# The recurrence's state enters the PSUM sum through a product with the identity, instead of a scaled copy on ScalarE

## Chip, core and metric

The kernel runs on one core of one Trainium2 chip. The metric is the device time of one execution in microseconds (us), the median of several runs. PE is TensorE's matmul, PEld its weight load, DVE is VectorE, ACT is ScalarE, POOL is GpSimd, SP is SyncE.

## What is computed

One layer of a hybrid decoder over 1024 prompt tokens and 8 single-token samples: norm, one input projection, a pooling mixer and an RWKV-7 recurrence side by side, one output projection, norm, a squared-ReLU MLP, a final norm. The part that matters here is the recurrence, for each of 8 heads of 64 x 64 state:

```
def step(S, inp):
    r_t, w_t, k_t, v_t, aa_t, bb_t = inp
    sa = jnp.einsum('bhvk,bhk->bhv', S, aa_t)
    S = S * w_t[:, :, None, :] + sa[..., None] * bb_t[:, :, None, :] + v_t[..., None] * k_t[:, :, None, :]
    return S, jnp.einsum('bhvk,bhk->bhv', S, r_t)
S_final, y = lax.scan(step, S0, xs)
```

## The kernel before

The prompt is worked in units: a unit is a pair of heads (`hp`, 0 to 3) in one half of the tokens (512), so 8 units. For each unit `rkv` projects the keys, receptances and values (line 185, tile `pj`: products in a high and a low part, three matmuls for each), `stage1` (S) makes the decays and the score matrices (line 431, tile `sc`), `inverse` (I) inverts the eight 64 x 64 triangular matrices of the unit's chunks by DVE, a trip through DRAM (`blk`, `inv`, `TX`) and small PE products (lines 548 to 570, tile `pi`) into `TT`, and `chain` (C) runs the recurrence itself: 8 chunks of 64 tokens, one after the other, 64 chunk steps in the whole kernel.

A chunk step in `chain` (lines 592 to 617 of the listing) goes through four engines in turn. `SV` holds for each head the state in one half of the partitions and the values in the other.

- PE, line 601: `pq` = AR x SV; line 602 starts the output sum `py`.
- ACT, `act(Q, pq)`: copies `pq` to SBUF.
- PE, line 605: `pa` = TT x Q.
- ACT, `act(SV[R[h], c, h, :], pa...)`, twice: puts the result over the state in SV.
- PE, line 608: `pu` = BKT x SV (the same PSUM columns as `pq`); line 609 ends `py`.
- DVE, line 617, twice: the next state = `pu` x gam + `sg`, written into the next chunk's SV.

`sg`, the old state times the chunk's decay `gam`, is made by ACT at the head of the step (line 596), before the state is overwritten. Products of full fp32 operands, as all of these, are two weight loads and two matmuls each on PE.

A Tile scheduler puts the instructions of all stages in an order on each engine, by priorities and by its own estimate of the costs; `lead_chain` gives the chain a lead of 600 places in that order. Each engine then runs its list strictly in order. So projections of later units stand between the products of a chunk step on PE. SP issues the loads in its own order (`TX` is the inverse on its way back, `mr` loads the mixer's rows for the output projection), POOL's queue issues the weights and the stores of mixer rows. After the last unit come the decode step, the output projection (`mx`, line 185 again) and the MLP.

Of the kernel before, what the change touches and what calls it, by code (L numbers as in the profile page):

```python
# [7 lines left out]
F32 = mybir.dt.float32  # L8
F32R = mybir.dt.float32r
AF = mybir.ActivationFunctionType  # L10
ALU = mybir.AluOpType
# [4 lines left out]
P = 128  # L16
# [70 lines left out]
def _build(ctx, nc, tc, I, O, dbg):  # L87
    V, A, PE, SY, GP = nc.vector, nc.scalar, nc.tensor, nc.sync, nc.gpsimd
# [4 lines left out]
    def act(out, in_, func=AF.Copy, bias=0.0, scale=1.0, **k):  # L93
        A.activation(out, in_, func, bias=bias, scale=scale, **k)  # L94

    def open_pool(stack, name, bufs=1, **k):
        return stack.enter_context(tc.tile_pool(name=name, bufs=bufs, **k))

    R = (slice(0, 64), slice(64, 128))
# [13 lines left out]
    ident = cst[:, C_ID:C_ID + 128]  # L113
# [77 lines left out]
    rcp = open_pool(st_left, "rcp", reuse_waits="tile")  # L191
# [386 lines left out]
    def chain(U):  # L578
        hp = U.hp
        z1 = Zt[U.half][2]  # L580
        for i in range(2):
            nm = f"{hp}_{2 * U.half + i}"
            AR, RB, BKT, SV, TT = U.AR[i], U.RB[i], U.BKT[i], U.SV[i], U.TT
            if i == 0:
                for h in range(2):
                    if U.half == 0:
                        GP.memset(SV[R[h], 0, h, :], 0.0)
                    else:
                        act(SV[R[h], 0, h, :], Sf[hp][R[h], :])
            pyp = ps_y.tile([P, 512], F32, tag="y", name=f"py{nm}")  # L590
            py = pyp.rearrange("p (c h t) -> p c h t", h=2, t=64)
            for c in range(4):
                g = 4 * i + c
                gn = f"{U.nm}_{g}"
                sg = rcp.tile([P, 2, 64], F32, tag="sg", name=f"sg{gn}", bufs=2)
                act(sg, SV[:, c, :, :], scale=U.gam[:, g:g + 1])

                o = 256 * (hp % 2)
                pq, pa = (pcs[:, o + 128 * q:o + 128 * q + 128].rearrange("p (h t) -> p h t", t=64) for q in range(2))
                pu = pq  # L600
                PE.matmul(pq, AR[:, c, 0, :, :], SV[:, c, :, :], start=True, stop=True)  # L601
                PE.matmul(py[:, c, :, :], SV[:, c, :, :], AR[:, c, 1, :, :], start=True, stop=False)
                Q = rcp.tile([P, 2, 64], F32, tag="Q", name=f"Q{gn}", bufs=2)
                act(Q, pq)
                PE.matmul(pa, TT[:, g, :, :], Q, start=True, stop=True)  # L605
                for h in range(2):
                    act(SV[R[h], c, h, :], pa[R[h], h, :])
                PE.matmul(pu, BKT[:, c, :, :], SV[:, c, :, :], start=True, stop=True)  # L608
                PE.matmul(py[:, c, :, :], SV[:, c, :, :], RB[:, c, :, :], start=False, stop=True)
                for h in range(2):  # L610
                    if g == 7:
                        dst = Sf[hp][R[h], :]
                    elif c == 3:
                        dst = U.SV[1][R[h], 0, h, :]
                    else:
                        dst = SV[R[h], c + 1, h, :]
                    V.scalar_tensor_tensor(dst, pu[R[h], h, :], U.gam[R[h], g:g + 1], sg[R[h], h, :], ALU.mult, ALU.add)
            ys = rcp.tile([P, 256], F32, tag="ys", name=f"ys{nm}", bufs=2)
            for h in range(2):
                act(ys[R[h]].rearrange("p (c t) -> p c t", t=64), py[R[h], :, h, :])  # L620
            post(hp, nm, pyp, ys, 256, U.bv[:, 256 * i:256 * i + 256], z1[:, 256 * i:256 * i + 256], ys)
            QM.dma_start(mix_d[4 + hp][U.half][:, 256 * i:256 * i + 256], ys)
        if U.half:
            QM.dma_start(O["wkv_p"][hp], Sf[hp])

    def post(hp, nm, ps, ys, n, bv, zg, out):

        pm, pv = ps[:, 256:512], ps[:, 0:256]
        PE.matmul(pm[:, :n], CJ, ys, start=True, stop=True)
        q = rcp.tile([P, 256], F32, tag="q", name=f"q{nm}", bufs=1)  # L630
        act(q[:, :n], pm[:, :n], AF.Square)
        PE.matmul(pv[:, :n], BO, q[:, :n], start=True, stop=True)
        act(q[:, :n], pv[:, :n], AF.Ln, bias=EPSG, scale=1.0 / 64)
        act(q[:, :n], q[:, :n], AF.Exp, scale=-0.5)
        V.tensor_tensor(out, pm[:, :n], q[:, :n], op=ALU.mult)
        V.scalar_tensor_tensor(out, out, col(V_LG, hp), bv, ALU.mult, ALU.add)
        pg = pm
        PE.matmul(pg[:, :n], glu[:, hp * P:(hp + 1) * P], zg, start=True, stop=True)
        V.scalar_tensor_tensor(out, out, col(V_LB, hp), pg[:, :n], ALU.add, ALU.mult)
# [184 lines left out]
    def lead_chain(U):  # L824
        with tc.high_priority(offset=LEAD):
            chain(U)
# [313 lines left out]
    for b in (1, 2):  # L1140
        c, n = BLK[b]
# [88 lines left out]
```

## Time and profile before

| | us |
|---|---|
| median of 3 runs (lowest, highest) | 1336.54 (1336.04, 1337.41) |
| the profiled execution | 1335.81 |
| its span in the trace | 1334.0 |
| busy in the span: PE, PEld, DVE, ACT | 1267.3, 1146.4, 1050.9, 822.5 |
| first and last chunk step in the span | 67.5 to 521 |

The table's busy times overlap each other. A matmul's end is modelled and neighbours overlap, so a PE that reads as busy can still have room; the distance from one weight load to the next is the better measure of what a product takes of PE's time. In the trace's rows a bracket behind an instruction says how long its engine had been idle before it and what ended that.

### The profile page before, as it was taken

The numbers are of one execution on the slowest core, as the hardware profiler recorded it, in microseconds if no ns is written. First come the engines' busy times: TensorE is split into PE (matmuls) and PEld (weight loads), VectorE is DVE, ScalarE is ACT, GpSimd is POOL, SyncE is SP. The second block draws the span as 40 slices with busy tenths as digits, with TensorE's granted clock in tenths as the row PEclk, the third lists the DMA queues.
The fourth block names the chain that finished last, engine by engine and source line by source line (L and its number), as shares of the span: only waits on it lengthen the run. The fifth ranks groups of instructions, "written<-read, shape, count | busy, mean of one in ns | idle before, by whom it ended". The sixth has DMA issues, their size and how long they took to land.

```text
span 1334.0 us, 27179 instructions
## 1 busy us (share of the span) xinstructions
PE 1267.3 (95%) x10230; PEld 1146.4 (86%) x10230; DVE 1050.9 (79%) x2331; ACT 822.5 (62%) x2015; POOL 125.4 (9%) x248
## 2 busy tenths in 40 slices
PE   5999999899999989989999999999899999999996
PEld 5987788798777867789989888998799999999996
DVE  8897687778877756589989997786698787878775
ACT  7668677776777657364757564555465645455552
POOL 4101001210011021110002320001000000000000
PEclk9999999999999989999999999999899999999999
DMA  6323123222222253442335663335634323332321
GB/s 209 102 54 83 43 50 90 95 93 53 66 56 48 63 164 135 142 149 80 119 115 150 181 167 96 113 97 186 217 99 147 103 89 105 94 106 93 104 71 64
DMA packets 119492, 143.19 MB, mean 107 GB/s; under 512 B 55769, under 2 KB 71257, under 8 KB 119353
## 3 DMA queue, kind: packets, MB, share of 16 engines
q1 hardware_dynamic: 97184, 92.22, 23.7%
q0 software_dynamic: 20320, 47.39, 11.4%
q10 hardware_dynamic: 1856, 1.85, 0.4%
q8 instruction: 80, 1.31, 0.4%
q14 instruction: 52, 0.42, 0.1%
HBM read 120.68 MB, written 20.97 MB: 106 GB/s over the span
## 4 chain that ended last, share of the span: by engine, by line
PE 68%; ACT 12%; DVE 11%; DMA 5%; issue 4%; POOL 1%; SPq 0%; DVEq 0%; ACTq 0%; POOLq 0%
PE dn L185 23%; PE b L1014 21%; PE pj L185 8%; PE mx L185 4%; ACT SV L94 2%; DMA a<-in_w_up 2%; PE pcs L608 1%; PE sc L431 1%; ACT wh L94 1%; ACT TT L94 1%; PE pcs L605 1%; DVE tm L525 1%; PE pcs L601 1%; DVE wl L167 1%; PE bkt L445 1%
## 5 line engine op out<-in xcount | busy, mean ns | idle before, releaser
L185 PE MATMUL dn<-uh,wh 128*128 128x260 f32 (+1 forms) x736 | 237.7, 324 | 6.1 <-DVE x L1080 4.3
L185 PE MATMUL dn<-ul,wh 128*128 128x260 f32 (+1 forms) x736 | 237.4, 323 | 1.2 <-DVE ul L1025 1.2
L185 PE MATMUL dn<-uh,wl 128*128 128x260 f32 (+1 forms) x736 | 237.2, 323 | 1.0 <-DVE wl L167 1.0
L94 ACT ACTIVATE wh<-a 128x512 fp32r<-128x512 f32 x192 | 120.8, 629 | 161.3 <-PE dn L185 85.0
L94 ACT ACTIVATE wh<-wr 128x512 fp32r<-128x512 f32 x230 | 142.9, 622 | 98.6 <-PE dn L185 26.0
L185 PE MATMUL pj<-xh,wh 128*128 128x258 f32 (+3 forms) x576 | 172.3, 299 | 13.7 <-ACT wh L94 13.7
L167 DVE TENSOR_TENSOR wl<-wr,wh 128x512 fp32r<-128x512 f32 x230 | 155.7, 681 | 35.4 <-ACT wh L94 27.5
L185 PE MATMUL pj<-xl,wh 128*128 128x258 f32 (+3 forms) x576 | 170.3, 296 | 0.0
L185 PE MATMUL pj<-xh,wl 128*128 128x258 f32 (+3 forms) x576 | 170.0, 295 | 0.1
L185 PEld LDWEIGHTS dn<-uh,wh 128*128 128x128 f32 x736 | 138.9, 189 | 17.3 <-ACT uh L94 3.2
L185 PEld LDWEIGHTS dn<-uh,wl 128*128 128x128 f32 x736 | 138.8, 189 | 12.3 <-DVE wl L167 1.2
L185 PEld LDWEIGHTS dn<-ul,wh 128*128 128x128 f32 x736 | 138.9, 189 | 10.8 <-DVE ul L1025 1.8
L176 DVE TENSOR_TENSOR wl<-a,wh 128x512 fp32r<-128x512 f32 x192 | 131.3, 684 | 6.2 <-ACT wh L94 3.6
L1080 DVE TENSOR_TENSOR x<-dn,x 128x260 f32<-128x260 f32 (+1 forms) x192 | 97.6, 511 | 41.5 <-PE dn L185 39.9
L185 PEld LDWEIGHTS pj<-xh,wh 128*128 128x128 f32 x576 | 109.9, 191 | 17.6 <-ACT wh L94 13.7
L185 PEld LDWEIGHTS pj<-xl,wh 128*128 128x128 f32 x576 | 110.0, 191 | 2.3 <-issue 1.9
L185 PEld LDWEIGHTS pj<-xh,wl 128*128 128x128 f32 x576 | 109.8, 191 | 1.8 <-issue 1.0
L94 ACT ACTIVATE c<-c 128x256 f32<-128x256 f32 (+1 forms) x128 | 53.1, 415 | 45.7 <-DVE c L1029 45.2
L991 DVE TENSOR_TENSOR a<-a,a 128x512 f32<-128x512 f32 x96 | 66.2, 689 | 19.0 <-DMA a<-in_w_up 17.5
L1025 DVE TENSOR_TENSOR ul<-u,uh 128x256 fp32r<-128x256 f32 (+1 forms) x128 | 53.6, 423 | 18.8 <-ACT uh L94 18.4
L185 PE MATMUL mx<-mh,wh 128*128 128x260 f32 (+1 forms) x192 | 64.9, 341 | 3.3 <-ACT mh L94 1.9
L185 PE MATMUL mx<-ml,wh 128*128 128x260 f32 (+1 forms) x192 | 63.6, 332 | 0.9 <-DVE ml L881 0.9
(421 smaller groups left out, 3388.6 us busy)
## 6 DMA issues: line engine op xcount, KB each, us to landing
a<-in_w_up SPq DMA_DIRECT2D x128, 256.0 KB, 2.6
wr<-in_w_down SPq DMA_DIRECT2D x128, 256.0 KB, 2.6
wr<-in_w_in POOLq DMA_DIRECT2D x72, 256.0 KB, 3.1
wr<-in_w_out POOLq DMA_DIRECT2D x26, 256.0 KB, 3.2
xr<-in_xT SPq DMA_DIRECT2D x16, 256.0 KB, 3.6
mr<-mix SPq DMA_DIRECT2D x8, 260.0 KB, 4.3
x<-in_xT SPq DMA_DIRECT2D x4, 520.0 KB, 5.0
blk<-AA SPq DMA_DIRECT2D x16, 128.0 KB, 2.7
```

Source lines behind the costliest of these rows:

```text
L94: A.activation(out, in_, func, bias=bias, scale=scale, **k)
L167: V.tensor_tensor(l[:, :w], raw[:, :w], f32(h[:, :w]), op=ALU.subtract)
L176: V.tensor_tensor(l, raw, f32(h), op=ALU.subtract)
L185: PE.matmul(ps, lhs, rhs, start=i == 0, stop=i == n - 1)
L431: PE.matmul(psc[:, c, :], BK[:, c, 2 * h:2 * h + 2, :], AR[:, c, :, h, :], start=True, stop=True)
L445: PE.transpose(pt[:, c, :], BK[:, c, 2 * h:2 * h + 2, :].rearrange("p a t -> p (a t)"), ident)
L525: V.tensor_tensor(pr[:, q], l[:, q].unsqueeze(2).to_broadcast([64, m, m, m]), r[:, q].rearrange("p k j -> p j k").unsqueeze(1).to_broadcas ...
L601: PE.matmul(pq, AR[:, c, 0, :, :], SV[:, c, :, :], start=True, stop=True)
L991: V.tensor_tensor(a[out], a[x], a[y], op=op)
L1014: PE.matmul(ps, lhs[:, c], rhs, start=k == i == 0, stop=k == 3 and i == 2)
L1025: V.tensor_tensor(ul, u, f32(uh), op=ALU.subtract)
L1080: V.tensor_tensor(d, ps[:, :n], d, op=ALU.add)
```

## The change

The scaled copy `sg` goes. In its place the old state is added into `pu` by PE, as a product with the identity that opens the sum, put between line 605 and the ACT writes that overwrite the state; the product with BKT continues the sum. DVE then multiplies the whole sum by `gam`: state x gam + pu x gam becomes (state + pu) x gam. The identity product also adds the other half of SV's rows (the values), in columns that DVE does not read.

```diff
-                sg = rcp.tile([P, 2, 64], F32, tag="sg", name=f"sg{gn}", bufs=2)
-                act(sg, SV[:, c, :, :], scale=U.gam[:, g:g + 1])
...
                 PE.matmul(pa, TT[:, g, :, :], Q, start=True, stop=True)
+                PE.matmul(pu, ident, SV[:, c, :, :], start=True, stop=False)
                 for h in range(2):
                     act(SV[R[h], c, h, :], pa[R[h], h, :])
-                PE.matmul(pu, BKT[:, c, :, :], SV[:, c, :, :], start=True, stop=True)
+                PE.matmul(pu, BKT[:, c, :, :], SV[:, c, :, :], start=False, stop=True)
...
-                    V.scalar_tensor_tensor(dst, pu[R[h], h, :], U.gam[R[h], g:g + 1], sg[R[h], h, :], ALU.mult, ALU.add)
+                    V.tensor_scalar(dst, pu[R[h], h, :], U.gam[R[h], g:g + 1], None, ALU.mult)
```

The scheduler orders all engines anew. Two lines are gone above, so that lines 601, 602, 605, 608 and 609 become 599, 600, 603, 607 and 608; the identity product is line 604 (the identity is a part of `cst`). On PE, from the product with TT of the sixth chunk of the second unit on, before:

```order
L605 MATMUL pcs<-Q_0_5_2007,TT_158 128x128
L185 MATMUL pj_0_2211<-xh_171,wl 128x256
L185 MATMUL pj_0_2211<-xh_171,wh 128x256
L185 MATMUL pj_0_2211<-xl_172,wh 128x256
L185 MATMUL pj_0_2211<-xh_171,wl 128x256
L608 MATMUL pcs<-SV_1_1268,BKT_1_1267 128x128
```

The same place on PE in the changed kernel:

```order
L603 MATMUL pcs<-Q_0_5_1992,TT_158 128x128
L604 MATMUL pcs<-SV_1_1268,cst 128x128
L185 MATMUL pj_1_2154<-xh_205,wh 128x258
L185 MATMUL pj_1_2154<-xl_206,wh 128x258
L185 MATMUL pj_1_2154<-xh_205,wl 128x258
L185 MATMUL pj_1_2154<-xh_205,wh 128x258
L607 MATMUL pcs<-SV_1_1268,BKT_1_1267 128x128
```

The identity product stands directly behind the product with TT, and as many projection matmuls (four) stand before the product with BKT as did before.

On ACT, at the head of the fifth chunk step of the first unit, before:

```order
L94 ACTIVATE ys_0_1350<-py_0_1297 64x256 x2
L94 ACTIVATE sg_0_4_1365<-SV_1_779,gam_0_669 128x128
L94 ACTIVATE Q_0_4_1369<-pcs 128x128
L94 ACTIVATE a_0_1651<-a_0_1651 128x512
L94 ACTIVATE q_0_1354<-py_0_1297 128x256
```

The same place on ACT in the changed kernel:

```order
L94 ACTIVATE ys_0_1346<-py_0_1297 64x256 x2
L94 ACTIVATE Q_0_4_1363<-pcs 128x128
L94 ACTIVATE a_0_1643<-a_0_1643 128x512
L94 ACTIVATE t_0_1657<-pk_0_1660,sm 128x512
L94 ACTIVATE q_0_1350<-py_0_1297 128x256
```

Q follows directly on what stood ahead of `sg`.

On SP, at the last unit's inverse, where the loads for the output projection begin (`inv` is the inverse's last store, `TX` its load), before:

```order
L538 DMA inv_162<-Es 32x16x16
L540 DMA TX_1_6001<-inv_162 128x8x64
L879 DMA mr_0_6514<-mix_0_70 128x512
L879 DMA mr_0_6520<-mix_0_72 128x512
L879 DMA mr_0_6526<-mix_0_74 128x512
```

The same place on SP in the changed kernel:

```order
L538 DMA inv_162<-Es 32x16x16
L878 DMA mr_0_6450<-mix_0_70 128x512
L878 DMA mr_0_6456<-mix_0_72 128x512
L540 DMA TX_1_5945<-inv_162 128x8x64
L878 DMA mr_0_6462<-mix_0_74 128x512
```

Two `mr` loads now stand ahead of `TX`.

## Rows read from the trace of the kernel before

**Rows 1.** The page: busy time, share of the span and instructions of each engine; and the chain of work that ended last, by engine.

```profile
PE 1267.3 (95%) x10230; PEld 1146.4 (86%) x10230; DVE 1050.9 (79%) x2331; ACT 822.5 (62%) x2015; POOL 125.4 (9%) x248
...
PE 68%; ACT 12%; DVE 11%; DMA 5%; issue 4%; POOL 1%; SPq 0%; DVEq 0%; ACTq 0%; POOLq 0%
```

**Rows 2.** Stretches of the recurrence: from and to, length, busy time of PE, PEld, DVE, ACT and POOL in us (instructions), granted clock of PE as a share of the full one, DMA share, GB/s.

```profile
110.00:200.00 90.00, 86.33 (x917) 71.46 (x917) 69.69 (x174) 66.39 (x189) 6.49 (x16) 1.00 0.21 50
200.00:300.00 100.00, 94.21 (x827) 83.45 (x828) 74.30 (x180) 75.08 (x209) 18.87 (x37) 1.00 0.31 93
300.00:400.00 100.00, 94.48 (x998) 80.79 (x997) 81.25 (x202) 73.41 (x206) 8.86 (x18) 1.00 0.24 59
...
460.00:530.00 70.00, 63.27 (x516) 49.89 (x517) 42.47 (x93) 45.15 (x143) 12.27 (x23) 0.93 0.44 141
```

**Rows 3.** One chunk step in order of time (start us, us, engine, line, operation; a bracket is the idle time before it): the step that begins at 407.88 and the head of the next.

```profile
407.88 0.30 PEld L601 LDWEIGHTS pcs<-SV,AR 128*128 128x128 f32 x2
...
408.10 0.30 PEld L602 LDWEIGHTS py<-AR,SV 128*128 128x128 f32 x2
...
408.32 0.19 PEld L185 LDWEIGHTS pj<-xl,wh 128*128 128x128 f32 x1
...
408.41 0.28 ACT L94 ACTIVATE Q<-pcs 128x128 f32<-128x128 f32 x1
408.43 0.19 PEld L185 LDWEIGHTS pj<-xh,wl 128*128 128x128 f32 x1
...
408.74 0.30 PEld L605 LDWEIGHTS pcs<-Q,TT 128*128 128x128 f32 x2
...
408.95 0.19 PEld L185 LDWEIGHTS pj<-xh,wh 128*128 128x128 f32 x1
...
409.26 0.45 ACT L94 ACTIVATE SV<-pcs 64x64 f32<-64x64 f32 x2 [0.58 <-PE pcs L605]
...
409.76 0.30 PEld L608 LDWEIGHTS pcs<-SV,BKT 128*128 128x128 f32 x2 [0.26 <-ACT SV L94]
...
410.59 0.57 DVE L617 SCALAR_TENSOR_TENSOR SV<-pcs,gam,sg 64x64 f32<-64x64 f32 x2
...
411.21 0.30 PEld L601 LDWEIGHTS pcs<-SV,AR 128*128 128x128 f32 x2
```

**Rows 4.** Waits of the weight loads between 60 and 530 us: who waited for whom, us in total, times, longest.

```profile
PEld pcs L608 <- ACT SV L94: 18.3, 50, 0.7
PEld pcs L605 <- ACT Q L94: 7.2, 26, 0.4
PEld pcs L601 <- DVE SV L617: 6.7, 16, 1.2
...
PEld py L629 <- ACT ys L94: 3.4, 10, 0.8
PEld pi L570 <- ACT Z L94: 3.3, 7, 0.8
```

**Rows 5.** Groups of instructions between 60 and 530 us: line, engine, operation, out<-in, shapes, count, busy us, mean ns, idle us before them and what ended it.

```profile
L617 DVE SCALAR_TENSOR_TENSOR SV<-pcs,gam,sg 64x64 f32<-64x64 f32 x112 | 31.7, 283 | 27.3 <-PE pcs L608 26.0
...
L94 ACT ACTIVATE SV<-pcs 64x64 f32<-64x64 f32 x128 | 27.6, 216 | 12.9 <-PE pcs L605 11.4
...
L94 ACT ACTIVATE sg<-SV,gam 128x128 f32<-128x128 f32 x64 | 25.0, 396 | 20.4 <-DVE SV L617 20.1
```

**Rows 6.** A chunk step of the first unit in order of time, with ACT late at its head.

```profile
118.99 0.77 ACT L94 ACTIVATE ys<-py 64x256 f32<-64x256 f32 x2
...
119.79 0.40 ACT L94 ACTIVATE sg<-SV,gam 128x128 f32<-128x128 f32 x1
...
120.21 0.28 ACT L94 ACTIVATE Q<-pcs 128x128 f32<-128x128 f32 x1
...
120.54 0.30 PEld L605 LDWEIGHTS pcs<-Q,TT 128*128 128x128 f32 x2 [0.43 <-ACT Q L94]
```

**Rows 7.** Groups of DVE instructions in the whole span, shapes apart (columns as in rows 5): those nearest in form to the new one.

```profile
L525 DVE TENSOR_TENSOR tm<-Xs,tw 64x64 f32<-64x64 f32 x16 | 3.6, 256 | 0.2
...
L144 DVE TENSOR_SCALAR da<-da 128x32 f32<-128x32 f32 x1 | 0.2, 182 | 0.0
```

**Rows 8.** Two stretches at the place where the projections run out (columns as in rows 2).

```profile
475.00:480.00 5.00, 0.58 (x65) 0.48 (x55) 0.69 (x1) 3.25 (x9) 0.33 (x1) 0.83 0.98 365
480.00:485.00 5.00, 5.00 (x41) 3.67 (x41) 3.69 (x7) 0.95 (x2) 0.54 (x1) 0.50 0.11 37
```

**Rows 9.** Instructions in order of time at that place (`po` is the pooling mixer's product, `pw` its weights).

```profile
469.73 0.38 SPq L540 DMA_DIRECT2D TX<-inv  x1
...
470.21 18.43 SPq L879 DMA_DIRECT2D mr<-mix  x7
...
471.71 0.74 PEld L783 LDWEIGHTS po<-d,pw 128*128 128x128 f32 x4
...
479.96 1.35 PEld L783 LDWEIGHTS po<-d,pw 128*128 128x128 f32 x4 [4.52 <-DMA pw<-in_pool_w]
...
481.42 0.34 PEld L185 LDWEIGHTS mx<-mh,wh 128*128 128x128 f32 x1
```

**Rows 10.** Loads between 470 and 482 us by kind: count, KB each, median us from issue to landing.

```profile
mr<-mix SPq DMA_DIRECT2D x5, 256.0 KB, 6.5
...
TX<-inv SPq DMA_DIRECT2D x1, 256.0 KB, 4.0
```

## The prediction

> **What bounds the kernel now.** I read the page first: PE is busy for 95% of the span and carries 68% of the chain that ended last, ACT only 12% [rows 1]. A change that takes work from ACT and gives it to PE starts on the wrong side of that. The MLP, behind 530 us, is not touched; so I read the stretches of the recurrence alone. From 200 to 400 us PE is busy for 94 of each 100 us, ACT for 73 to 75 [rows 2]: no engine is full but PE, and PE only nearly.
>
> Then one chunk step, to see what PE and the recurrence do to each other [rows 3]. The step is a ring PE, ACT, PE, ACT, PE, DVE. From the load for line 601 (407.88) to that for 605 (408.74) it takes 0.86 us, on to 608 (409.76) 1.02, on to the next 601 (411.21) 1.45: 3.33 us in all. Between them PE runs projection matmuls, and at 608 it still stands for 0.26 us until ACT has written SV. Over the recurrence these stops add up to 18.3 us at 608, 7.2 at 605 (waiting for Q) and 6.7 at 601 (waiting for the DVE write) [rows 4]. So PE is full except for short stops inside the ring, and the question is whether the new product falls into such a stop or lengthens the way.
>
> **What the change costs and gives, part by part.**
>
> *The identity product: 64 added.* It is a full 128 x 128 fp32 product like those of lines 602 and 605. What such a product takes of a loaded PE is the distance from its first weight load to the next instruction's: 408.10 to 408.32 for 602, 408.74 to 408.95 for 605, so 0.22 and 0.21 us [rows 3]; a projection matmul takes 0.11 there (408.32 to 408.43). I take 0.22: 64 x 0.22 = 14.1 us of PE time.
>
> Is it hidden? It stands between 605 and the projection matmuls, where PE is not waiting; the stop comes later, at 608. That stop ends when ACT has written SV, and this write now has to wait for the identity product too, since it overwrites the state which that product reads. In the step shown, the write would begin 0.22 us after 409.26, and PE, with the same four projection matmuls between, would come to 608 0.22 us later as well: the stop stays 0.26 and the whole step is 0.22 longer. The product hides nothing and is hidden by nothing. Bounds: 14.1 us as such; at the other end, if the 50 stops at 608 took up 0.2 us each, 14.1 - 10 = 4.1.
>
> *The scaled copy: 64 removed, 25.0 us of ACT* [rows 5]. ACT is not the bound, so only what it delays counts: Q. In the first step shown it delays nothing [rows 3]. In another ACT was late [rows 6], with `ys` until 119.76; then `sg` ran for 0.40 and Q could start only at 120.21, and PE stood for 0.43 at 605. Without `sg` Q would start at about 119.79 and nearly all of that goes. What can be won is at most the 7.2 us of the 26 stops at 605 [rows 4], at least nothing. Some of each stop is the plain length of the ring: in the first step ACT was on time with Q [rows 3], and still no weights were loaded from 408.62 (408.43 and 0.19) to 408.74. 26 x 0.12 = 3.1 remain, 4.1 are ACT's lateness, and ACT will now be late with other things in some of them. I take -3.
>
> *The DVE write: one input fewer, 128 of them.* Now 283 ns [rows 5]. The new form, a tensor times a column of scalars out of PSUM, is not in the trace. The nearest rows are a product of two 64x64 tensors, 256 ns, and a scalar operation on 128x32, 182 ns [rows 7]. So a step's two writes become shorter by 2 x 27 = 0.05 us, at best 2 x 101 = 0.20, at worst by nothing. It counts where PE stands at 601, 16 times [rows 4]: 16 x 0.05 = 0.8, at most 16 x 0.20 = 3.2. I take -1, nearer the row of the same size.
>
> [...]
>
> *Other things for which PE waits on ACT*: `ys` 3.4 us and Z 3.3 [rows 4]. 25 us less on an engine that is busy for three quarters moves these a little: 0 to -3, I take -1.
>
> *The scheduler's new order.* Rows of other stages trade places by a few, up and down, which I count at nothing. [...] Two of them now go out ahead of `TX`. That brings the output projection's rows sooner and the inverse later: `TX` landed in 4.0 us and may take the 6.5 of its neighbours [rows 10], 2.5 more, and as much again if they hold up its issue. [...] Between +5 and -7, I take 0.
>
> Sum: 14.1 - 3 - 1 - 1 + 0 = +9.1 us. Against the profiled execution's 1335.81 that is 1344.9; the median of the runs is 0.7 higher, so **1345.6** for the median.
>
> **The rivals.**
>
> *Nothing is won back (slower still).* ACT is in time with Q as often as before because the scheduler fills the gap with other work, the write is no shorter, and `TX`, now behind two loads of 256 KB, comes later by up to 5 us, PE standing idle for it: 14.1 + 5 = +19, so 1350 to 1356. For it: what made ACT late in the second step, `ys` [rows 6], still stands ahead of Q. Against it: `sg` stood ahead of every Q, and it is gone.
>
> *PE has room.* From 110 to 400 us the weight loads are busy for 71.46, 83.45 and 80.79 us of 90, 100 and 100 [rows 2], which leaves 54 us in which no weights were loaded; 14.1 would go in. The mechanism would be that the stops at 608 shrink by what the product adds, to the 4.1 us above, and with the -5 of the other terms the sum is -0.9: 1335 to 1339. For it: 18.3 us of stops at 608. Against it: the write that ends the stop waits for the product. [...]
>
> [...]
>
> **How the numbers follow.** Forecast (+5 to +14, 1341 to 1350.5): 0.62. Nothing won back (1350 to 1356): 0.18. PE has room (1335 to 1339): 0.12. Faster (about 1333): 0.08. A measurement of this kernel can tell about 0.2% (2.7 us) from no change. Faster by more than that: 0.08. Within: 0.09, nearly all of the third case. Slower: 0.83. The range of 8 in 10 leaves out the fast case, most of the room case and the end of the slow one: 1338 to 1354.
>
> **What would show it.** Right, if line 604 shows 128 weight loads with the next instruction 0.21 to 0.22 us behind each pair; if the stops at the product with BKT stay near 18 us in total (right: the product is not hidden) and do not fall to 8; if the stops for Q fall from 7.2 to about 4; if the DVE write reads 230 to 260 ns; and if the trace's stretches from 60 to 460 us are about 10 us longer in sum, with the MLP as long as before. Wrong, if the product's pair takes another time than 0.22, if the stops at 608 shrink, or if the difference stands where the projections run out [rows 8] instead of in the ring.

## The result, and the profile after

| | before | after |
|---|---|---|
| median, us (lowest, highest; 4 runs each) | 1336.88 (1336.04, 1337.41) | 1352.30 (1349.55, 1355.82) |
| the profiled execution, us | 1335.81 | 1355.82 |

The change makes the kernel slower by 15.4 us, ratio 1.0119, interval [1.0103, 1.0136]. The prediction said 1345.6 and +9.1: the right side and inside its range, but 6 us too small. The profiled execution of after is the slowest of its four, 3.5 us above the median, so its trace (span 1354.1 us against 1334.0) shows a few us more than there are to explain.

The page of after, against [rows 1]: busy time by engine, and the chain of work that ended last.

```profile
PE 1286.1 (95%) x10358; PEld 1163.4 (86%) x10358; DVE 1052.0 (78%) x2331; ACT 805.7 (60%) x1951; POOL 125.2 (9%) x248
...
PE 66%; DVE 11%; ACT 10%; issue 6%; DMA 5%; POOL 1%; DVEq 0%; SPq 0%; POOLq 0%; ACTq 0%
```

ACT loses 16.8 us (the copies were 25.0 [rows 5]; neighbouring instructions overlap on ACT too: in before their times sum to 899.9 us for the 822.5 that ACT is busy), PE's weight loads gain 17.0 and its matmuls 18.8, 128 of each. DVE's time is what it was.

One chunk step of after in order of time, to be laid beside [rows 3]: with 599, 600, 603, 607, 608 for 601, 602, 605, 608, 609, the identity product on line 604, and the DVE write on line 616 for 617.

```profile
408.59 0.30 PEld L599 LDWEIGHTS pcs<-SV,AR 128*128 128x128 f32 x2 [0.17 <-DVE SV L616]
...
408.81 0.30 PEld L600 LDWEIGHTS py<-AR,SV 128*128 128x128 f32 x2
...
409.18 0.28 ACT L94 ACTIVATE Q<-pcs 128x128 f32<-128x128 f32 x1 [0.26 <-PE pcs L599]
...
409.50 0.30 PEld L603 LDWEIGHTS pcs<-Q,TT 128*128 128x128 f32 x2 [0.17 <-ACT Q L94]
...
409.72 0.30 PEld L604 LDWEIGHTS pcs<-SV,cst 128*128 128x128 f32 x2
...
409.95 0.19 PEld L185 LDWEIGHTS pj<-xl,wh 128*128 128x128 f32 x1
410.06 0.19 PEld L185 LDWEIGHTS pj<-xh,wl 128*128 128x128 f32 x1
410.18 0.19 PEld L185 LDWEIGHTS pj<-xh,wh 128*128 128x128 f32 x1
410.25 0.45 ACT L94 ACTIVATE SV<-pcs 64x64 f32<-64x64 f32 x2 [0.80 <-PE pcs L604]
410.31 0.19 PEld L185 LDWEIGHTS pj<-xl,wh 128*128 128x128 f32 x1
...
410.75 0.30 PEld L607 LDWEIGHTS pcs<-SV,BKT 128*128 128x128 f32 x2 [0.26 <-ACT SV L94]
...
411.28 0.58 DVE L616 TENSOR_SCALAR SV<-pcs,gam 64x64 f32<-64x64 f32 x2 [2.75 <-PE pcs L607]
```

Read from load to load: 603 to 607 takes 1.25 us, where 605 to 608 took 1.02. The identity product holds PE for 0.23 (409.72 to 409.95), four projection matmuls follow as before, and PE then stands 0.26 us for SV, exactly as long as before. That is the prediction's picture to the hundredth. The other end is not: Q starts the moment its product ends, no `sg` is in the way, and PE still stands 0.17 us for it.

Waits of the weight loads of after between 60 and 545 us (who for whom, us in total, times, longest), against [rows 4]; the window is longer because the recurrence is.

```profile
PEld pcs L607 <- ACT SV L94: 18.1, 56, 0.7
PEld pcs L603 <- ACT Q L94: 7.8, 28, 0.7
PEld po L782 <- ACT mh L94: 6.5, 1, 6.5
...
PEld pcs L599 <- DVE SV L616: 3.7, 16, 0.7
...
PEld pi L570 <- ACT Z L94: 2.4, 5, 0.9
PEld py L628 <- ACT ys L94: 2.1, 7, 0.4
```

Groups of after in the same window, against [rows 5].

```profile
L616 DVE TENSOR_SCALAR SV<-pcs,gam 64x64 f32<-64x64 f32 x112 | 31.7, 283 | 33.0 <-PE pcs L607 31.6
...
L94 ACT ACTIVATE SV<-pcs 64x64 f32<-64x64 f32 x128 | 27.7, 217 | 21.5 <-PE pcs L604 20.4
...
L94 ACT ACTIVATE Q<-pcs 128x128 f32<-128x128 f32 x64 | 17.7, 276 | 24.9 <-PE pcs L599 23.8
```

ACT now idles for 24.9 us ahead of the 64 Qs (4.0 before), yet the stops for Q are 7.8 us, not fewer. In before `sg` was what ACT ran directly ahead of Q at 18 of the 26 stops; in after it is other work at all 28: `wh` (the high part of a weight) at 6, `BKT` and `SV<-vt` at 4 each. If Q is called late when it starts over 0.2 us behind the (modelled) end of its product, it was late at 15 of 26 stops, with 4.7 of the 7.2 us, and is late at 13 of 28, with 4.8 of the 7.8. And the DVE write with one input less takes 283 ns, as with two.

Where the time went: PE's busy time up to the last weight load of a projection, and from there to the last `mx` product (columns as in [rows 2]). Before:

```profile
0.00:471.60 471.60, 437.19 (x4233) 379.81 (x4234) 371.49 (x919) 341.62 (x920) 67.78 (x141) 1.00 0.29 79
471.60:626.90 155.30, 142.00 (x1031) 118.18 (x1030) 109.99 (x251) 85.25 (x241) 20.39 (x37) 0.97 0.43 140
```

After:

```profile
0.00:485.90 485.90, 452.44 (x4345) 394.71 (x4346) 370.97 (x919) 326.64 (x863) 67.12 (x141) 0.99 0.28 76
485.90:644.40 158.50, 145.82 (x1045) 120.86 (x1045) 109.69 (x251) 83.38 (x234) 20.86 (x38) 0.95 0.44 139
```

The first part is 14.3 us longer: PE busy +15.2 (weight loads +14.9), PE idle 34.4 before and 33.5 after. So the whole product is there, and all the relief of ACT has taken 0.9 us from PE's idle time. The second part is 3.2 us longer, and what follows 2.6 (707.1 before, 709.7 after), in an execution 3.5 us above its median.

The place where the projections run out, against [rows 8, 9], in windows (columns as in [rows 2]); first ten us of before, where the five of [rows 8] are the second half, then after:

```profile
470.00:480.00 10.00, 4.32 (x150) 3.65 (x148) 2.99 (x7) 5.67 (x15) 3.22 (x6) 0.91 0.90 290
```

```profile
485.00:490.00 5.00, 2.13 (x15) 1.66 (x13) 2.43 (x6) 1.97 (x5) 3.22 (x6) 0.92 0.93 198
490.00:495.00 5.00, 1.78 (x5) 1.50 (x5) 1.86 (x4) 1.73 (x3) 0.00 (x0) 0.50 1.05 349
495.00:500.00 5.00, 5.00 (x74) 3.42 (x72) 3.45 (x6) 2.21 (x5) 1.09 (x2) 0.50 0.58 203
```

and the loads of PE there in order of time, the inverse's first product (line 548) in before, then after:

```profile
473.75 0.63 PEld L548 LDWEIGHTS pi<-TX,AA 16*32 16x32 f32 x64 [1.29 <-DMA TX<-inv]
```

```profile
485.97 0.74 PEld L782 LDWEIGHTS po<-d,pw 128*128 128x128 f32 x4
493.19 1.35 PEld L782 LDWEIGHTS po<-d,pw 128*128 128x128 f32 x4 [6.48 <-ACT mh L94]
494.65 0.33 PEld L185 LDWEIGHTS mx<-mh,wh 128*128 128x128 f32 x1
...
497.78 0.94 PEld L548 LDWEIGHTS pi<-TX,AA 16*32 16x32 f32 x64 [0.65 <-issue]
```

PE idles for 6.1 of the ten us from 485 and then runs 5 us and more at a granted clock of 0.50. In before it idled for 5.7 of the ten from 470, with one window of five at 0.50 behind [rows 8]. The place is no better and a little worse. The load's row puts the second `po`'s wait down to ACT's `mh`, which ended at 492.90. The matmul's own group names the weights `pw`:

```profile
L782 PE MATMUL po<-d,pw 128*128 128x256 f32 (+1 forms) x32 | 11.2, 467 | 6.1 <-DMA pw<-in_pool_w 6.1
```

They were issued at 487.43 and took 5.7 us to land, until 493.1: PE waited for weights, as in before. What changed places is the inverse. `TX` took 6.1 us to land (4.0 before [rows 10]), and the first product that reads it started 12.3 us behind the issue of the inverse's last store (485.44), where it was 6.8 in before (466.91).

### The profile page after: what moved, and what is told of

Read it like the earlier page. It is cut to its first block, busy times and chain, and to the rows that moved or that the text cites. A ratio compares the mean times of both kernels' runs of the same rounds, so it can differ in the third digit from the quotient of the medians.

```text
span 1354.1 us, 27397 instructions
## 1 busy us (share of the span) xinstructions
PE 1286.1 (95%) x10358; PEld 1163.4 (86%) x10358; DVE 1052.0 (78%) x2331; ACT 805.7 (60%) x1951; POOL 125.2 (9%) x248
## 4 chain that ended last, share of the span: by engine, by line
PE 66%; DVE 11%; ACT 10%; issue 6%; DMA 5%; POOL 1%; DVEq 0%; SPq 0%; POOLq 0%; ACTq 0%
PE dn L185 20%; PE b L1013 18%; PE pj L185 9%; PE mx L185 4%; PE pcs L607 2%; DMA a<-in_w_up 2%; ACT SV L94 2%; PE sc L431 2%; PE pcs L603 1%; ACT wh L94 1%; PE pcs L599 1%; DVE tm L525 1%; ACT TT L94 1%; DVE wl L167 1%; PE py L608 1%
```

## The experiments

Two theories stood at the start. **P**: PE's work is the bound, so each product costs its own slot wherever it stands, and a shorter way round the ring wins little. **R**: the ring is the bound (the write over the state has to wait for the product), so a product beside the ring would be nearly free. The expectations of e1 and e2 set **G** against P: a product costs more than its slot (19 to 20 us for 64), and the removal of the copy wins some 5 back. Later **T** was added: part of the cost is a tail, because the last unit's inverse comes late. Each run is measured against the kernel before on the same chip; us is the ratio's distance from 1 times the median of before (1336.6 to 1338.1); on that scale the change is +15.9.

| run | ratio [interval] | us |
|---|---|---|
| e1_no_identity | 0.9980 [0.9966, 0.9994] | -2.7 |
| e2_add_gating | 1.0143 [1.0120, 1.0165] | +19.1 |
| e3_add_free | 1.0141 [1.0122, 1.0161] | +18.9 |
| e4_add_behind | 1.0097 [1.0077, 1.0117] | +13.0 |
| e5_add_ungated | 1.0156 [1.0141, 1.0172] | +20.9 |
| e6_longer_ring | 0.9984 [0.9972, 0.9996] | -2.1 |
| e7_copy_on_dve | 0.9973 [0.9959, 0.9987] | -3.6 |
| e8_copy_on_pool | 1.0017 [1.0005, 1.0029] | +2.3 |
| e9_scores_early | 1.0087 [1.0068, 1.0105] | +11.6 |
| e10_before_scores_early | 0.9972 [0.9960, 0.9984] | -3.7 |
| e11_dve_scores_early | 0.9953 [0.9936, 0.9969] | -6.3 |

**e1: the copy's removal alone.** The changed kernel without line 604; the old state's share of the sum is left out.

```diff
-                PE.matmul(pu, ident, SV[:, c, :, :], start=True, stop=False)
-                PE.matmul(pu, BKT[:, c, :, :], SV[:, c, :, :], start=False, stop=True)
+                PE.matmul(pu, BKT[:, c, :, :], SV[:, c, :, :], start=True, stop=True)
```

> The changed kernel without the identity product: the old state's share is left out of the sum, so that neither the scaled copy on ScalarE nor anything in its place is computed. Theory P (the 14 us are the products' own time on PE, 64 x 0.22, and removing the copy gains nothing): 1352.3 - 14 = about 1338, the same as before within 3. Theory G (the products cost more than their slots, about 19 to 20, and removing the copy wins some 5 back, as the prediction's terms have it): about 1332. Stops for Q at the product with TT: P about 7 us, G about 4.

Its waits from 60 to 545 us:

```profile
PEld pcs L606 <- ACT SV L94: 16.9, 50, 0.7
PEld pcs L599 <- DVE SV L615: 7.4, 21, 1.0
PEld pcs L603 <- ACT Q L94: 6.1, 23, 0.5
```

Everything that the change gives, without what it costs, is 2.7 us (0.8 to 4.5), not 5. The time of 1334.2 lies between G (1332) and P (1338). The stops for Q fall by 1.1 us against [rows 4], not by 3, and those for the DVE write rise.

**e2: the product alone.** Kernel before, `sg` kept; the product's sum is overwritten by the next one.

```diff
                 PE.matmul(pa, TT[:, g, :, :], Q, start=True, stop=True)
+                PE.matmul(pu, ident, SV[:, c, :, :], start=True, stop=True)
```

> The kernel before, scaled copy kept, with the identity product of the state added behind the product with TT; the product with BKT opens the sum anew. So ScalarE and VectorE do what they did and PE has 64 products more, and the write over the state must wait for them. Theory P: before + 14 = about 1351, like the changed kernel. Theory G: about 1356, some 5 above the changed kernel, since the copy is still there.

```profile
PEld pcs L609 <- ACT SV L94: 18.3, 49, 1.2
PEld pcs L605 <- ACT Q L94: 6.2, 20, 0.8
```

+19.1 (16.0 to 22.1), more than the 14.1 of its slots, while the stops keep their size: 1356.3 us, as G said, and not the 1351 of P. With e1 this gives 19.1 - 2.7 = +16.4, close to the +15.9 of the change itself: the two halves add up.

**e3: the same product with another operand,** RB in place of the state, at the same place.

```diff
+                PE.matmul(pu, ident, RB[:, c, :, :], start=True, stop=True)
```

> As the run with the added products, at the same place on PE, but the identity multiplies RB instead of the state, so that the write over the state need not wait for it. Theory P (PE's slots count): the same as that run, about 1351. Theory R (the ring counts: the write waits 0.22 us longer in each step): the products fill PE's stops at the product with BKT, these fall from 18 to about 8 us, and the time is about 1341.

This did not do what it was meant to. ACT's write over the state still waited for the product, as its group shows:

```profile
L94 ACT ACTIVATE SV<-pcs 64x64 f32<-64x64 f32 x126 | 27.3, 217 | 22.6 <-PE pcs L606 21.3
```

`pu` and `pa` are columns of one tile, `pcs`, and the write reads that tile. So +18.9 says nothing on P against R.

**e4: the same product behind line 609,** in columns that ACT has read by then.

```diff
                 PE.matmul(py[:, c, :, :], SV[:, c, :, :], RB[:, c, :, :], start=False, stop=True)
+                PE.matmul(pa, ident, RB[:, c, :, :], start=True, stop=True)
```

> As the run with the added products on RB, but they stand behind line 609, out of the way of everything in the step but the next step's product, which waits for VectorE anyway. Theory P: before + 14, about 1350. Theory R: the ring is not longer, PE's stops take the products up, 1337 to 1342.

```profile
L618 DVE SCALAR_TENSOR_TENSOR SV<-pcs,gam,sg 64x64 f32<-64x64 f32 x112 | 31.7, 283 | 23.5 <-PE pcs L610 19.8 <-PE vt L449 2.1
L94 ACT ACTIVATE SV<-pcs 64x64 f32<-64x64 f32 x128 | 27.7, 216 | 13.2 <-PE pcs L605 11.7
```

The write over the state is free of it now, but the DVE write waits for it (line 610). +13.0 (1350.3 us, as P said), the cheapest place, and still nearly a full slot.

**e5: a product for which no link of the ring waits,** with a stationary of zeros into the output sum's tile. The scheduler puts it ahead of the product with TT, where PE stops for Q.

```diff
+                PE.matmul(py[:, c, :, :], ZW, RB[:, c, :, :], start=False, stop=False)
```

> Kernel before with its scaled copy kept, and in each of the 64 chunk steps one more 128x128 fp32 product (a stationary of zeros times the restart tile, so that it adds zero) into the accumulator of the output, ahead of the two-term product, where TensorE often stops for the decayed queries. The write over the state does not wait for it. Theory P (TensorE has no room in the step, a slot is a slot): 64 x 0.22 = 14 us, 1350 to 1353 us. Theory R (what costs is the chain state write - product - eviction, and a product that fills a stop is absorbed by it): 4 to 8 us, 1341 to 1346 us, and the stops for the queries fall from 7 to under 4 us.

Its waits from 60 to 545 us, and its group for ACT's write:

```profile
PEld pcs L610 <- ACT SV L94: 18.6, 51, 1.6
...
PEld pcs L606 <- ACT Q L94: 5.3, 16, 0.6
...
PEld pcs L602 <- DVE SV L619: 4.9, 13, 1.2
```

```profile
L94 ACT ACTIVATE SV<-pcs 64x64 f32<-64x64 f32 x124 | 26.9, 217 | 18.4 <-PE pcs L606 17.1
```

The write waits for the TT product, not for the added one, and the kernel is slower by 20.9 all the same: 1358.2 us, far above R's range and above P's too. R falls. 14 us of work placed right ahead of a wait of 7.2 us took 1.9 off that wait. Where the rest went can be counted in the traces: in before, 605's load follows 602's directly in 4 of the 64 steps; here the TT product follows the added one directly in 25. Other work had stood in that gap, and the scheduler moved it out to make room. An estimate (each load at the median distance to the next for its kind, over the steps with at most nine such loads in the gap) gives 18.4 us of other work in 54 steps of before and 8.6 in 55 of e5: 9.8 less, where 49 added products, 10.9 us of slots, had come in. The way from 602's load to 605's did not grow: 0.68 us a step before and 0.69 here. The work moved out still has to be done, and that is the price.

**e6: a longer ring without more work on PE.** e1 with ACT's first write made once more (the expectation says twice more; the edit and the trace have one, 64 in all); as in e1, the old state's share is left out.

```diff
-                for h in range(2):
+                for h in (0, 1, 0):
                     act(SV[R[h], c, h, :], pa[R[h], h, :])
```

> The changed kernel without its identity product (the old state's share is left out, as in e1_no_identity, 1334.2 us), with ScalarE's write of the first state matrix made twice more per chunk step: some 0.2 us more in the chain of each step that needs it, no work more on TensorE. Theory R (chain): up to 14 us above e1, 1344 to 1348 us, with the stops for the state write rising from 17 to about 30 us. Theory P (TensorE's slots bound the step): 1334 to 1337 us.

```profile
PEld pcs L606 <- ACT SV L94: 24.8, 59, 1.0
```

```profile
L94 ACT ACTIVATE SV<-pcs 64x64 f32<-64x64 f32 x192 | 41.6, 217 | 19.8 <-PE pcs L603 16.1
```

ACT's writes in the ring are longer by 41.6 - 27.7 (e1) = 13.9 us, the stops for the write grow from 16.9 to 24.8, and the kernel goes from 0.9980 to 0.9984 of before: 0.5 us, and by the two intervals at most some 3 (in the two profiled executions PE idles for 3.8 us more up to the last projection). This is the counterpart of e5: of 14 us in the ring little or nothing shows in the time, 14 us of PE work cost all of it and more. The stops are what the scheduler's order leaves, not what sets the time.

**e7 and e8: the copy on VectorE, on GpSimd.**

```diff
-                act(sg, SV[:, c, :, :], scale=U.gam[:, g:g + 1])
+                V.tensor_scalar(sg, SV[:, c, :, :], U.gam[:, g:g + 1], None, ALU.mult)
```

(`GP` in place of `V` for e8.)

> Kernel before with the scaled copy of the state made by VectorE in place of ScalarE. The run without the copy and without the product bounds what can be won at about 3 us. If VectorE's added 0.2 us per step lies in its idle time: 1334 to 1337 us; if it stands ahead of the eviction that the next product waits for: 1340 to 1350 us.

> Kernel before with the scaled copy of the state made by GpSimd. If GpSimd is free then: 1334 to 1337 us, with the stops for the queries at 6 us as in e1. If the copy lies behind transfers that GpSimd issues, the state's eviction waits for it: 1345 us or more.

e7's waits from 60 to 545 us, then its group for the copy:

```profile
PEld pcs L608 <- ACT SV L94: 14.1, 44, 0.6
PEld pcs L605 <- ACT Q L94: 6.5, 26, 0.6
PEld pcs L601 <- DVE SV L617: 5.1, 16, 0.7
```

```profile
L596 DVE TENSOR_SCALAR sg<-SV,gam 128x128 f32<-128x128 f32 x64 | 17.7, 280 | 0.8 <-ACT SV L94 0.4
```

and e8's:

```profile
L596 POOL TENSOR_SCALAR sg<-SV,gam 128x128 f32<-128x128 f32 x64 | 54.4, 851 | 136.7 <-DVE SV L617 116.8 <-ACT SV L94 19.4 <-POOL SV L587 0.2
```

On VectorE the copy takes 280 ns where ACT takes 396, and the kernel gains 3.6 us, all that e1 allows. ACT's freedom for Q is not where it comes from: the stops for Q are 6.5 us (7.2 before), those at the BKT product 14.1 (18.3); why they fall was not tested. On GpSimd the copy takes 851 ns and costs 2.3 us, 1338.9, between the two ranges expected.

**e9, e10, e11: the tail.** In the changed kernel the second chunk step of the last unit started 27.6 us behind the last projection (513.5 and 485.9), in before 19.1 (490.7 and 471.6). The edit raises the priority of the last unit's scores, in the changed kernel (e9, offset 100), in before (e10, offset 300) and in e7 (e11, 300).

```diff
-        if c[0] in calls:
+        if c == "S7":
+            with tc.high_priority(offset=100):
+                stage1(units[7])
+        elif c[0] in calls:
```

> The changed kernel with one edit: stage 1 of the last unit (its scores) gets a higher priority, so that TensorE's program holds more of the last projections behind these scores. Theory T (part of the cost is a tail: the last inverse is ready later than the projections run out, so the last unit's recurrence starts late): in the changed kernel the second chunk step of the last unit comes 27.6 us behind the last projection and the last mx product 158.5 us behind it, 19.1 and 155.3 in the kernel before; here the first falls to 10 to 18 us, the second to 153 to 155 us, and the time to 1347 to 1350 us. Rival (the two only go together; all the cost is the product's slots): 1351 to 1354 us whatever the order.

> Kernel before with the last unit's scores given a higher priority, as in e9. Theory T: its tail has some 2 us left to win (second chunk step of the last unit from 19 to some 14 us behind the last projection): 1334 to 1336 us. If the step up costs elsewhere (scores ahead of an older unit's recurrence): 1337 to 1342 us.

> Kernel before with the scaled copy on VectorE (e7_copy_on_dve: 0.9973 of before) and the last unit's scores given a higher priority. If the two add up: 1331 to 1333 us, ratio 0.995 to 0.997; if not, as e7.

e9 gave the time that T expected, 1349.4 us. The step moved further than meant: 486.2, now 11.1 us ahead of the last projection (497.3). Without e10 that would have passed for proof. But before gains 3.7 us by the same lever (its step goes from 490.7 to 476.6, 2.5 us ahead of its last projection), and with both in the early order the change costs 1.0087 / 0.9972 = 1.0115, as much as the 1.0119 without. Up to the last `mx` product, e9 and then e10 (columns as in [rows 2]):

```profile
0.00:638.40 638.40, 596.19 (x5388) 514.64 (x5389) 482.41 (x1169) 410.54 (x1097) 88.11 (x178) 0.99 0.33 93
```

```profile
0.00:621.20 621.20, 577.34 (x5260) 497.34 (x5261) 479.55 (x1169) 425.96 (x1161) 88.32 (x178) 1.00 0.34 95
```

e9 is 17.2 us longer, with PE busy +18.9 and idle -1.7; after against before it was 17.5, +19.1 and -1.6. So the tail is a loss of both kernels, and no part of the change's price can be seen in it. e11 joins both gains: 1331.49 us, 0.9953 [0.9936, 0.9969], faster than both kernels.

## Why the prediction was right in sign and short in size

*The product, +14.1.* Right in kind and nearly in size. Line 604's pair is followed by the next load after 0.223 us (the median of 64), the stops at the BKT product stayed (18.3, now 18.1), the step shown grew by 0.23 from TT to BKT, and up to the last projection PE is busy for 15.2 us more. The reason given, that the write over the state must wait for it, is true but is not what decides: e5's product delays no write and cost no less. It is not hidden because the scheduler's order already has other work in nearly every gap of the ring (in before between 605 and 608 in all 64 steps, between 602 and 605 in 60).

Alone the product cost 13.0 to 20.9 us by its place (e4 to e5). The traces show what that spread is made of. Up to the last `mx` product, with PE's busy time at a granted clock of 0.50 counted at half (an estimate; a projection's load is followed by the next after 0.12 us at the full clock and 0.21 there, medians in after), the six traces with the product have 586 to 590 us of PE work and the seven without it 570 to 576; the means differ by 15.0 (slots: 14.1). The rest is PE's idle time (47.7 us before, 42.3 in e4, 50.8 in e5) and its time at 0.50 (10.2, 20.5, 23.9). Why these came out so in each order was not settled.

*What the change gives back, -3, -1 and -1.* This is the step that failed, the -3 for Q above all. All of it together measured -2.7 (e1), and in the changed kernel PE's idle time up to the last projection fell by 0.9. "The stops for Q fall from 7.2 to about 4": they are 7.8. Taking 4.1 of the 7.2 us as ACT's lateness was near the mark (4.7 by the count above). What failed is that most of it would go with `sg`: the new order put other ACT work in its place, and Q is as late as before (4.8 us; 3.1 in e1). The prediction allowed for that "in some of them"; it was in nearly all. Nor did the stops for a Q on time fall (2.5, now 3.0): there is a little less other work between 600 and 603 (by the estimate used for e5 0.30 us a step, 0.34 before), so PE comes to 603 earlier and waits there. The stops for `ys` and Z did fall, by 2.2 us (6.7, now 4.5), more than the 1 taken; PE's idle time as a whole did not follow.

*The DVE write, -1 (down to -3.2).* Zero: 283 ns with and without the second tensor input. The nearest row, 256 ns [rows 7], had both inputs in SBUF; the better neighbour was the old write itself, which reads the same PSUM tile.

*The place where the projections run out, 0.* Nothing was won there. The -7 between which and +5 the 0 was taken was an estimate that no run shows: PE idled there for 6.1 of ten us, 5.7 in before, with two windows of five at 0.50 behind, where before had one. `mr` loads went ahead of `TX` as foreseen, and the second `po` still waits for its weights: 6.48 us in one piece, where before had 4.52 [rows 9] and 1.8 more around the inverse's first products, which now come behind it. In this execution the stretch from the last projection on is 3.2 us longer, but e9 and e10 show that the whole difference stays when the order there is changed.

*The sum.* Slots 15.1 (the distances behind line 604 summed, some of them at the lower clock) less the 2.7 of e1 is 12.4; 15.4 was measured. The missing 3 us are about what the two intervals leave open (0.8 to 4.5 for e1, 13.8 to 18.2 for the change). In the traces they stand in PE's busy time (+19 up to the last `mx`, in both pairs), not in its waits, and there they are the clock: up to that product PE ran at 0.50 for 23.9 us in after and 10.2 in before, 13.7 in e9 and 3.4 in e10. With busy time at 0.50 counted at half, the +19.1 and +18.9 become +13.5 and +13.9. Whether the change brings the lower clock or these executions happened to have it stays open: e7, with no product added, ran at 0.50 for 30.7 us up to there.

*The rivals.* "Nothing is won back" (1350 to 1356, at 0.18) came nearest: 1352.3 lies in its range and outside that of the favoured case (1341 to 1350.5). Two of its three reasons hold: ACT is late with Q as often as before because other work fills the gap, and the write is no shorter. Its third, a late `TX`, came true as such (6.1 us to land; its first use 5.5 us later behind the inverse's last store), but PE does not stand idle for it: 12.7 us from the last projection to the last `mx`, 13.3 before. "PE has room" fell with e5 (+20.9 us for 14.1 of slots): weight loads were busy 81 of the 100 us from 300 to 400 [rows 2], and next to nothing of the other 19 could be had by adding a product.

## What to carry to other kernels

Where, as here, a scheduler fills the gaps of a dependent chain with other work, a wait on the busiest engine is what its order leaves over, not room: price work added to that engine at its full slot even if it lands in a wait (here 13.0 to 20.9 us for 14.1 of slots), and work taken from the other engines at next to nothing (here 2.7 us for 25.0 of ACT). To tell the two apart, add a product on which nothing depends, and lengthen the chain without adding work. And give the kernel before every lever that you pull in the changed one: e9 alone confirmed a cause that e10 took away.

## What the runs showed of the hardware

- A DVE read of 64x64 fp32 from PSUM took 283 ns as a product with a column of scalars (after, line 616) and 283 as the same plus a tensor from SBUF (before, line 617 [rows 5]); the second input added nothing here. A 128x128 scaling from SBUF to SBUF, twice the columns on twice the partitions, took 280 (e7).
- That scaling took 280 ns on VectorE (e7), 396 on ScalarE [rows 5] and 851 on GpSimd (e8).
- A 128x128 fp32 product, two weight loads, held PE for 0.223 us to the next weight load, on lines 600, 604 and 608 of after alike (medians of 64 each).
- Up to the last `mx` product PE ran at the lower granted clock (0.50) for 3.4 us (e10) to 30.7 us (e7), by execution. The distance between a projection's loads was 0.12 us at the full clock and 0.21 at 0.50 (medians in after).
